# Score products in two phases, GpSimd's work in layer 0 moved, v and a gate product in native float32

## The chip, the core and the metric

One core of a Trainium2 chip runs the kernel. The metric is device time in microseconds (us) of one launch. Five queues work beside each other: TensorE (products, written to the accumulator banks), VectorE, ScalarE and GpSimd (elementwise work) and SyncE (DMA from main memory).

## What is computed

Two layers on 256 tokens of width 1,024, all float32. Layer 0 mixes tokens by an RWKV-7 recurrence, layer 1 by causal attention; each is followed by a dense gated network and each sub-layer by a LayerNorm. The change touches layer 0's mixer:

```
xx = time_shift(x) - x
xr, xw, xk, xv, xa, xg = [x + xx * mu[n] for n in range(6)]
r, k, v = xr @ w_r, xk @ w_k, xv @ w_v
w = -softplus(-(w0 + tanh(xw @ w1) @ w2)) - 0.5
a = sigmoid(a0 + (xa @ a1) @ a2)
g = sigmoid(xg @ g1) @ g2
kk = k * k_k, each head divided by its norm
k = k * (1 + (a - 1) * k_a)
per token: S = S * decay + (S @ -kk) kk*a + v k ;  y = S @ r
out = (group_norm(y) + bonus(r, k, v)) * g @ w_o
```

## The kernel before

The recurrence runs in four chunks of 64 tokens. Within a chunk all pairs of tokens meet in score matrices: for each of the 16 heads, keys and removal keys (tile `KB`, 128 columns: 64 of each) are multiplied with the scaled `-kk` and the scaled r (tile `AR`, 64 columns of each). The part with `-kk` is a triangular matrix that must be inverted before the recurrence can begin. `scores(q)` (line 876) makes both parts in one product of 128 columns per head and chunk, sixteen per group q of four heads. VectorE multiplies each bank with the causal mask into `SC`, and ScalarE copies the 32-wide diagonal blocks to `LD`. It begins when `KB` is whole (`kb`), and r has been scaled (`ar`).

`inverse` (line 951) waits for all `ld` events, transposes `LD` to `LT` on VectorE and then runs 31 short steps of a product `tmp` and a sum `TT`. It ends with the transposes `TN` and `LD`. `merge` (line 996) builds 64-wide inverses out of the 32-wide ones by small TensorE products named `n` and `t`. Between the two it asks `fill` for a number of v products (lines 1000 to 1020); with `FREE = 10` the first of these requests is met only after eleven of the sixteen parts of v's second half. Then `recurrence` (line 1036) runs steps z, u, s and y per chunk and half of the heads. `stacked` builds `AZ`, `bonus` scales `v` on GpSimd with the bonus sums `sb`.

Float32 weights go through `Stream` (line 101) in tiles of 128 rows by 1,024. A "split" tile is loaded into one of three `raw` buffers, rounded by ScalarE to `hi`, and its rest `lo` is taken by VectorE or GpSimd; a product is then three fast ones (hi with hi, lo with hi, hi with lo). Table `PL` (line 69) says which tiles' `lo` go to GpSimd. A "native" tile is loaded into a slot and multiplied as float32 directly, slower per column but with no split. "stack" is a smaller split, and "raw" a native tile that lies in a raw buffer.

```
OFF = ('ka', 'kk1', 'xxv')
PL = {..., 'k': [2], 'r': [0], 'v': [2, 3, 4, 5, 6, 7], 'g2': [0, 1], ...}
MIXV = 'pool'
MIXG = 'pool'
for n, (ww, xx) in enumerate(((w[0], xh), (w[1], xh), (w[0], xl))):
    mm(ps, xx[:, k % 4, TOK[hf]], ww[:, kk, :], ...)
```

These are OFF, the operations that GpSimd has in layer 0 (the scaling `ka` in `weigh`, one half of `KB` in `keys`, the rest of the split of xv), and who makes the inputs xv and xg in `mix` (line 649), and `v_part` (line 1222), the three products of v. The gate's second product has four products per block of 128 columns, 32 in all.

The order on every queue is set when the program is built. `Issue.run` (line 357) plays the program on `Clock` (line 197), a table of costs per engine; of the parts that are ready by it, the one with the lowest rank goes next. `dense0` (line 1259), the row of large products k, r, v, g and o, has rank 30, the last. So a change of a cost, of a rank or of the work moves instructions everywhere. Each engine then executes its instructions strictly in this order.

Of the kernel before, what the change touches and what calls it, by code (L numbers as in the profile page):

```python
# [99 lines left out]

class Stream:
# [29 lines left out]
    def run(self):  # L131
        for i, (name, kind, a, b, rows, src) in enumerate(self.specs):
# [61 lines left out]
class Clock:  # L194


    def __init__(self):
# [42 lines left out]
    def charge(self, eng, op, args, kw):  # L240
# [9 lines left out]
        elif eng == "PE":  # L250
# [8 lines left out]
            late = 0.197
        elif eng == "DVE":  # L260
            cost, late = 0.068 + n / (1920.0 if op == "tensor_scalar" and not psum else 960.0) * (6 if op == "reciprocal" else 1), 0.128
            cost += 0.0625 * sum(x.free_size() == 1 for x in srcs if n > 1)
# [1517 lines left out]
```

## Time and profile before

| what | value |
|---|---|
| median of 3 runs | 745.94 us (743.14 to 745.95) |
| the profiled execution | 744.11 us, its span 742.3 us |
| busy TensorE, VectorE, ScalarE, GpSimd | 684.7, 535.8, 389.8, 186.9 us |
| share of the chain of waits, TensorE, VectorE, ScalarE | 66%, 21%, 4% |
| mean granted TensorE clock | 0.967 of 2.4 GHz |

The busy time of TensorE holds waits inside its pipeline, so 92% busy doesn't say that it bounds everything; which engine bounds a stretch is read from the chain of waits and from the idle time in front of single rows. All rows carry line 300, a helper; the names of the tiles tell the operation. Times of a row are from the span's start.

### The profile page before, as it was taken

The numbers are of one execution on the slowest core, as the hardware profiler recorded it, in microseconds if no ns is written. First come the engines' busy times: TensorE is split into PE (matmuls) and PEld (weight loads), VectorE is DVE, ScalarE is ACT, GpSimd is POOL, SyncE is SP. The second block draws the span as 40 slices with busy tenths as digits, with TensorE's granted clock in tenths as the row PEclk, the third lists the DMA queues.
The fourth block names the chain that finished last, engine by engine and source line by source line (L and its number), as shares of the span: only waits on it lengthen the run. The fifth ranks groups of instructions, "written<-read, shape, count | busy, mean of one in ns | idle before, by whom it ended". The sixth has DMA issues, their size and how long they took to land.

```text
span 742.3 us, 11807 instructions
## 1 busy us (share of the span) xinstructions
PE 684.7 (92%) x4500; PEld 585.5 (79%) x4500; DVE 535.8 (72%) x912; ACT 389.8 (53%) x711; POOL 186.9 (25%) x132
## 2 busy tenths in 40 slices
PE   6899797898878999999999699999979999999995
PEld 5799796777657888888888478777769888888885
DVE  7989999839997756655666935977686656666576
ACT  5864445465344555455456424756636554545560
POOL 5677956451462100000000713113040000000000
PEclk9989889899999999999999999999999999999998
DMA  6445213030545655555557615345056555555541
GB/s 243 153 143 192 90 47 114 30 115 33 174 168 187 226 194 178 196 190 185 192 191 216 233 48 179 126 142 200 28 170 197 189 188 194 180 189 197 179 164 57
DMA packets 33577, 117.21 MB, mean 158 GB/s; under 512 B 3808, under 2 KB 4832, under 8 KB 33520
## 3 DMA queue, kind: packets, MB, share of 16 engines
q1 hardware_dynamic: 31936, 110.89, 44.6%
q10 hardware_dynamic: 1584, 5.57, 2.3%
q8 instruction: 35, 0.57, 0.3%
q14 instruction: 22, 0.18, 0.1%
HBM read 115.40 MB, written 1.05 MB: 157 GB/s over the span
## 4 chain that ended last, share of the span: by engine, by line
PE 66%; DVE 21%; ACT 4%; issue 4%; DMA 2%; POOL 1%; DVEq 0%; SPq 0%; ACTq 0%; POOLq 0%
PE gu L300 29%; PE acc L300 14%; PE qkv L300 9%; DVE xtok L300 3%; DVE TT L300 3%; PE gn L300 2%; DVE lo L300 2%; DVE tmp L300 2%; PE o L300 2%; PE sc L300 2%; DVE xlo L300 1%; DVE mx L300 1%; PE tr L300 1%; PE k L300 1%; POOL lo L300 1%
## 5 line engine op out<-in xcount | busy, mean ns | idle before, releaser
L300 DVE TENSOR_TENSOR lo<-raw,hi 128x1024 fp32r<-128x1024 f32 (+1 forms) x172 | 210.7, 1231 | 151.4 <-ACT hi L300 151.0
L300 ACT CAST hi<-raw 128x1024 fp32r<-128x1024 f32 (+1 forms) x214 | 212.1, 999 | 175.7 <-issue 75.9
L300 PE MATMUL gu<-xw,hi 128*128 128x512 f32 x640 | 225.9, 393 | 0.0
L300 PE MATMUL gu<-xw,lo 128*128 128x256 f32 x640 | 180.3, 282 | 0.0
L300 POOL TENSOR_TENSOR lo<-raw,hi 128x1024 fp32r<-128x1024 f32 (+1 forms) x41 | 89.0, 2185 | 245.2 <-ACT hi L300 232.7
L300 PEld LDWEIGHTS gu<-xw,hi 128*128 128x128 f32 x640 | 120.1, 188 | 26.5
L300 PEld LDWEIGHTS gu<-xw,lo 128*128 128x128 f32 x640 | 120.3, 188 | 0.8
L300 PE MATMUL acc<-hi,hh 128*128 128x512 f32 (+1 forms) x180 | 53.7, 368 | 0.0
L300 PE MATMUL acc<-lo,hh 128*128 128x512 f32 (+1 forms) x180 | 53.7, 368 | 0.0
L300 PE MATMUL acc<-hi,hl 128*128 128x512 f32 (+1 forms) x180 | 53.6, 367 | 0.0
L300 PE MATMUL qkv<-hi,xhi 128*128 128x512 f32 x96 | 39.5, 412 | 0.5 <-ACT xhi L300 0.5
L300 ACT ACTIVATE silu<-silu 128x256 f32<-128x256 f32 x40 | 16.7, 417 | 44.0 <-DVE silu L300 44.0
L300 PE MATMUL qkv<-hi,xlo 128*128 128x512 f32 x96 | 38.0, 396 | 0.6 <-DVE xlo L300 0.6
L300 PE MATMUL qkv<-lo,xhi 128*128 128x512 f32 x96 | 38.1, 396 | 0.0
L300 PEld LDWEIGHTS acc<-hi,hl 128*128 128x128 f32 x180 | 32.7, 188 | 6.3 <-DVE hl L300 0.2
L300 PEld LDWEIGHTS acc<-lo,hh 128*128 128x128 f32 x180 | 32.7, 188 | 5.8
L300 PEld LDWEIGHTS acc<-hi,hh 128*128 128x128 f32 x180 | 31.7, 188 | 6.0 <-ACT hh L300 0.2
L300 PE MATMUL o<-hi,xhi 128*128 128x512 f32 x64 | 27.7, 436 | 2.8 <-ACT xhi L300 2.8
L300 PE MATMUL o<-lo,xhi 128*128 128x512 f32 x64 | 27.1, 423 | 2.0 <-POOL lo L300 2.0
L300 PE MATMUL o<-hi,xlo 128*128 128x512 f32 x64 | 27.0, 428 | 0.9 <-DVE xlo L300 0.9
L300 POOL TENSOR_TENSOR ro<-ro 128x512 f32<-128x512 f32 x8 | 12.1, 1513 | 55.9 <-DVE ro L300 55.9
L300 PE MATMUL gn<-hi,xw 128*128 128x256 f32 x128 | 24.8, 290 | 0.1
(229 smaller groups left out, 1291.4 us busy)
## 6 DMA issues: line engine op xcount, KB each, us to landing
raw<-in_w_in_dram SPq DMA_DIRECT2D x80, 512.0 KB, 3.4
raw<-in_w_dn_dram SPq DMA_DIRECT2D x44, 512.0 KB, 3.4
raw<-in_w_qkv_dram SPq DMA_DIRECT2D x24, 512.0 KB, 3.3
raw<-in_w_o_dram SPq DMA_DIRECT2D x20, 512.0 KB, 3.4
raw<-in_w_r_dram SPq DMA_DIRECT2D x8, 512.0 KB, 3.5
raw<-in_w_v_dram SPq DMA_DIRECT2D x8, 512.0 KB, 3.6
raw<-in_w_if_dram SPq DMA_DIRECT2D x8, 512.0 KB, 3.3
raw<-in_w_k_dram SPq DMA_DIRECT2D x6, 512.0 KB, 3.8
```

The costliest lines, as they stand in the source:

```text
L300: ins = f(*args, **kw).ins
```

## The change

Seven edits, all for layer 0 up to the recurrence, and new costs in the planner.

1. `scores(q, n)` has two phases. Phase 0 needs only `KB` and the `-kk` part of `AR`. It makes products of 64 columns into two banks, with the two halves of rows in turn, feeds `LD` and is masked into `SC`. Phase 1 multiplies with r's part, into a tile of its own, `SR`, which only step y reads. Ranks are 3 and 5.
2. `OFF` is empty. Both halves of `KB` are VectorE's, and `ka` is an activation with scale and bias on ScalarE.
3. Inputs xv and xg are made on VectorE, eight steps of 256 elements each (on GpSimd it was eight operations of 512 for each).
4. v's weights are native: the first half in raw buffers, the second in `lo` buffers. xv isn't split.
5. The gate's second product is native, with one block of 128 and one of 32 rows (before, 96 rows held the 32 three times). Its activations aren't split.
6. The splits of k and r on GpSimd go to VectorE. `selrk` is one operation instead of eight.
7. The planner prices the port that VectorE and GpSimd share, a change of the number of rows on TensorE, scans and fast products differently.

```
-OFF = ('ka', 'kk1', 'xxv')
+OFF = ()
 MIXR = 'dve'
 MIXA = "dve"
 BON = 'pool'
 BONW = 'T'
 ORDERED = False
-PL = {'wo1': [5, 6, 7], 'in1': [0, 1, 2, 3], 'qkv': [1, 3, 4, 5, 6, 7, 11], 'wo0': [1, 2, 4, 6, 7, 9, 10], 'k': [2], 'r': [0], 'v': [2, 3, 4, 5, 6, 7], 'g2': [0, 1], 'w2': [], 'in0': [0, 2, 3, 5]}
+PL = {'wo1': [5, 6, 7], 'in1': [0, 1, 2, 3], 'qkv': [1, 3, 4, 5, 6, 7, 11], 'wo0': [1, 2, 4, 6, 7, 9, 10], 'in0': [0, 2, 3, 5]}
 LD = {}
-MIXV = 'pool'
-MIXG = 'pool'
+MIXV = 'dve'
+MIXG = 'dve'
...
+NATIVE = ("native", "in hi", "in lo")
...
+            elif kind in NATIVE:
+                raw = self.wp.tile([128, 1024], F32R, tag=kind[3:], name=f"nat{i}", bufs=SPL).bitcast(F32)
...
-                cols, cost = n, n / 2388.0
+                cols, cost = n, n / 2388.0 + 0.014
             else:
-                cols, cost = 4 * n, max(n / 588.0, m / 600.0) if not beside else max(0.027, m / 1200.0)
+                rows = self.region(aps[1])[1][:2]
+                turn = rows[1] - rows[0] <= 64 and self.rows not in (None, rows)
+                self.rows = rows
+                cols, cost = 4 * n, max(n / 588.0, m / 600.0) if not beside and not turn else max(0.027, m / 1200.0)
             late = 0.197
+            k = aps[1].partition_size()
+            shape = 32 if k <= 32 else 64 if k <= 64 else 128
+            if self.shape not in (None, shape):
+                cost += SWITCH
+            self.shape = shape
...
+            wide = [x for x in srcs if x.free_size() > 1 or n == 1]
+            if eng == "POOL" and op != "memset" or eng == "DVE" and not psum and (
+                    len(wide) > 1 or op in ("tensor_scalar", "tensor_copy")):
+                start = self.shared(eng, start, cost)
...
-    s2("v", "w_v", 0)
+    s2("v", "w_v", 0, "raw")
     s1("g1", "w_g1a", 0, "native")
-    s1("g1", "w_g1b", 0, "native", 96)
-    specs.append(("g2", "split", 1, 1024, 128, a["w_g2a"]))
-    specs.append(("g2", "stack", 1, 1024, 96, a["w_g2b"]))
-    s2("v", "w_v", 1)
+    s1("g1", "w_g1b", 0, "native", 32)
+    specs.append(("g2", "in hi", 1, 1024, 128, a["w_g2a"]))
+    specs.append(("g2", "in hi", 1, 1024, 32, a["w_g2b"]))
+    s2("v", "w_v", 1, "in lo")
...
-            on("ka").tensor_scalar(w[:, j, :], av[g][:, o + j, :], vec[:, KA + p:KA + p + 1], omka[:, p:p + 1],
-                              ALU.mult, ALU.add)
+            act.activation(w[:, j, :], av[g][:, o + j, :], AF.Identity, scale=vec[:, KA + p:KA + p + 1],
+                           bias=omka[:, p:p + 1])
+        yield w
+        yield I.idle("DVE")
...
-    def scores(q):
+    def scores(q, n):
 
         yield ev(f"kb{q}")
-        yield ev(f"ar{q}")
-        yield ev("SC")
-        fin = count(4, lambda: I.reach(ev(f"sc{q}"), SC[:, :, q * 2:q * 2 + 2]))
-        left = count(4, lambda: I.reach(ev(f"ld{q}"), LD))
-
-        def done(j, hp, ps):
-            for d in range(2):
-                r, h = 64 * (1 - hp) + 32 * d, (q * 2 + j) * NC
-                act.copy(out=LD[r:r + 32, h:h + NC, :],
-                         in_=ps[r:r + 32].rearrange("p (c t) -> p c t", c=NC)[:, :, 32 * d:32 * d + 32])
-            left()
-            dve.tensor_tensor(SC[:, hp, q * 2 + j], ps.rearrange("p (c t) -> p c t", c=NC),
-                              mask[:, None, :].to_broadcast([128, NC, 128]), ALU.mult)
+        if n == 1:
+            yield ev(f"ar{q}")
+        yield ev(("SC", "SR")[n])
+        dst = (SC, SR)[n]
+        fin = count(2, lambda: I.reach(ev(f"{('sc', 'sr')[n]}{q}"), dst[:, :, q * 2:q * 2 + 2]))
+        left = count(2, lambda: I.reach(ev(f"ld{q}"), LD))
+
+        def done(hp, ps):
+            if n == 0:
+                for d in range(2):
+                    r = 64 * (1 - hp) + 32 * d
+                    act.copy(out=LD[r:r + 32, q * 8:q * 8 + 8, :],
+                             in_=ps[r:r + 32].rearrange("p a c t -> p (a c) t")[:, :, 32 * d:32 * d + 32])
+                left()
+            dve.tensor_tensor(dst[:, hp, q * 2:q * 2 + 2], ps,
+                              mask[:, None, None, n * C:n * C + C].to_broadcast([128, 2, NC, C]), ALU.mult)
             fin()
 
+        ps = [bank("sc").rearrange("p (a c t) -> p a c t", a=2, c=NC) for _ in HALF]
         for j in range(2):
-            for hp in range(2):
-                rs = HALF[hp]
-                ps = bank("sc")
-                for c in range(NC):
-                    mm(ps[:, c * 128:(c + 1) * 128], KB[q][rs, j, c].rearrange("p o t -> p (o t)"),
-                       AR[q][rs, j, c].rearrange("p o t -> p (o t)"), True, True)
-                I.after(ps, done, j, hp, ps)
-                yield 0.0
+            for c in range(NC):
+                for hp, rs in enumerate(HALF):
+                    mm(ps[hp][:, j, c, :], KB[q][rs, j, c].rearrange("p o t -> p (o t)"), AR[q][rs, j, c, n, :], True, True)
+        for hp in range(2):
+            I.after(ps[hp], done, hp, ps[hp])
...
+            for q in (2 * f, 2 * f + 1):
+                yield ev(f"sr{q}")
...
-                mm(y[vr, ds], SC[:, hp, p, c, 64:128], UV[c][:, hp, p, :], start=(c == 0), stop=True,
+                mm(y[vr, ds], SR[:, hp, p, c, :], UV[c][:, hp, p, :], start=(c == 0), stop=True,
...
-            xh, xl = mixed["xv"][k // 4]
-            for n, (ww, xx) in enumerate(((w[0], xh), (w[1], xh), (w[0], xl))):
-                mm(ps, xx[:, k % 4, TOK[hf]], ww[:, kk, :], start=(k + n == 0), stop=(k + n == KT + 1))
+            mm(ps, mixed["xv"][k // 4][:, k % 4, TOK[hf]], w[:, kk, :], start=(k == 0), stop=(k == KT - 1))
...
-        x = half_slot("sg")[:rows, 0, :]
-        act.activation(x, ps[:rows, :T], AF.Sigmoid)
-        yield x
-        act.copy(out=hgs[:rows, n * 2, :], in_=x)
-        yield hgs[:rows, n * 2, :]
-        if n == 0:
-            dve.tensor_tensor(hgs[:, 1, :], x, hgs[:, 0, :].bitcast(F32), ALU.subtract)
-        else:
-            dve.tensor_tensor(hgs[32:64, 2, :], x[32:64], hgs[32:64, 2, :].bitcast(F32), ALU.subtract)
-        I.reach(ev(f"hg{n}"), hgs[:rows, n:n * 2 + 1, :] if n else hgs[:, 0:2, :])
+        act.activation(hgs[:rows, n, :], ps[:rows, :T], AF.Sigmoid)
+        I.reach(ev(f"hg{n}"), hgs[:rows, n, :])
...
-                mix(3, "xv", 3, slot, eng=dict(pool=pool, dve=dve)[MIXV])
-        early.close()
-        scp = l0.enter_context(tc.tile_pool(name="scp", bufs=1))
-        SC = scp.tile([128, 2, KT, NC, 128], F32, name="SC")
-        SCh = SC.rearrange("p a h c t -> p a (h c) t")
-        LD = scp.tile([128, 32, 32], F32, name="LD")
-        I.reach(ev("SC"))
+                mix(3, "xv", 3, eng=dict(pool=pool, dve=dve)[MIXV])
+        early_r.close()
+        srp = l0.enter_context(tc.tile_pool(name="srp", bufs=1, side="right"))
+        SR = srp.tile([128, 2, KT, NC, C], F32, name="SR")
+        I.reach(ev("SR"))
...
-                for n, (ww, xx_) in enumerate(((g2[0][0], hgs[:, 0, :]), (g2[0][1], hgs[:, 0, :]), (g2[0][0], hgs[:, 1, :]),
-                                               (g2[1][0], hgs[:96, 2, :]))):
-                    mm(ps[:, j * T:(j + 1) * T], ww[:, 0, p * 128:(p + 1) * 128], xx_, start=(n == 0), stop=(n == 3))
+                for n, rows in enumerate((128, 32)):
+                    mm(ps[:, j * T:(j + 1) * T], g2[n][:, 0, p * 128:(p + 1) * 128], hgs[:rows, n, :], n == 0, n == 1)
...
-        for p in range(KT):
-            pool.tensor_scalar(selrk[:, p, :], sel2, vec[:, RK + p:RK + p + 1], None, ALU.mult)
+        pool.tensor_tensor(selrk, sel2[:, None, :].to_broadcast([128, KT, 2]),
+                           vec[:, RK:RK + KT, None].to_broadcast([128, KT, 2]), ALU.mult)
...
-        I.add(4, scores(q))
+        I.add(3, scores(q, 0))
+        I.add(5, scores(q, 1))
```

`shared`, called there, delays the one engine in the plan while the other holds the port.

How the order moves, at the three places that the prediction speaks of:

VectorE at the start of the inverse. `SC` and `SR` are masks, `AR` and `rk` are r's rows, `mix` is xv. Before:

```order
L300 TENSOR_TENSOR SC<-sc_1096,cst 128x512
L300 TENSOR_TENSOR SC<-sc_1104,cst 128x512
L300 STREAM_TRANSPOSE LT_165<-LD 128x32x32
L300 TENSOR_TENSOR tmp<-LT_165,TT_166 128x31
L300 TENSOR_TENSOR TT_166<-TT_166,tmp 128x31
L300 TENSOR_TENSOR tmp<-LT_165,TT_166 128x60
L300 TENSOR_TENSOR TT_166<-TT_166,tmp 128x2x30
```

With the change:

```order
L337 TENSOR_TENSOR SC<-sc_904,cst 128x512
L337 TENSOR_TENSOR SC<-sc_905,cst 128x512
L337 TENSOR_TENSOR rk_991<-r_705,k_119 128x512
L337 STREAM_TRANSPOSE LT_168<-LD 128x32x32
L337 TENSOR_TENSOR AR_125<-r_806,G_117 128x8x64
L337 TENSOR_TENSOR tmp<-LT_168,TT_169 128x31
L337 TENSOR_TENSOR rk_1029<-r_806,k_120 128x512
L337 TENSOR_TENSOR TT_169<-TT_169,tmp 128x31
L337 SCALAR_TENSOR_TENSOR mix_1025<-xx_110,vec,xT_84 128x256
L337 TENSOR_TENSOR tmp<-LT_168,TT_169 128x60
```

In all eight masks precede `LT`; before there were sixteen. Rows of r and of xv now stand between the steps of the inverse, and further down so do `SR` and xg.

TensorE between the inverse and the recurrence: `n` and `t` belong to the merge, `hg` is the gate's activation. Before, the end of the gate's product:

```order
L300 MATMUL g_1441<-hg_151,hi_1304 128x256
L300 MATMUL g_1441<-hg_151,hi_1273 128x256
L300 MATMUL g_1441<-hg_151,lo_1274 128x256
L300 MATMUL g_1441<-hg_151,hi_1273 128x256
L300 MATMUL n_1421<-TN_167,SC 32x32 x16
L300 MATMUL n_1422<-TN_167,SC 32x32 x32
L300 MATMUL g_1441<-hg_151,hi_1304 128x256
L300 MATMUL v_1543<-hi_1343,xhi_865 128x512
L300 MATMUL v_1543<-lo_1344,xhi_865 128x512
L300 MATMUL v_1543<-hi_1343,xlo_866 128x512
L300 MATMUL v_1543<-hi_1343,xhi_865 128x512
L300 MATMUL n_1421<-TN_167,SC 32x32 x16
```

With the change, the same place:

```order
L337 MATMUL g_1349<-mix_1203,nat_1224 32x256 x4
L337 MATMUL g_1349<-mix_1204,nat_1224 32x256 x4
L337 MATMUL n_1363<-TN_170,SC 32x32 x16
L337 MATMUL n_1364<-TN_170,SC 32x32 x32
L337 MATMUL g_1443<-hg_154,nat_1226 128x256
L337 MATMUL n_1363<-TN_170,SC 32x32 x16
L337 MATMUL g_1443<-hg_154,nat_1228 128x256
L337 MATMUL g_1443<-hg_154,nat_1226 128x256
L337 MATMUL g_1443<-hg_154,nat_1228 128x256
```

The gate's second product stood ahead of the first `n` but for its last row; now all sixteen of its products stand behind the first 48 of `n`. Eleven native v products follow and then the first `t`.

ScalarE before the decay `G`: `E` and `a` are sigmoids, `kkr` is the scaled k. Before:

```order
L300 ACTIVATE a_109<-z_346,vec 128x256 x2
L300 ACTIVATE a_109<-z_353,vec 128x256 x2
L300 ACTIVATE a_110<-z_360,vec 128x256 x2
L300 ACTIVATE sq_375<-kkr_118 128x512
L300 CAST hi_386<-raw_265 128x1024
L300 ACTIVATE a_110<-z_367,vec 128x256 x2
L300 ACT_TABLE_LOAD
L300 ACTIVATE G_113<-E_111 128x16x64
```

With the change:

```order
L337 ACTIVATE sq_361<-kkr_121 128x512
L337 CAST hi_376<-raw_261 128x1024
L337 ACTIVATE a_113<-z_353,vec 128x256 x2
L337 CAST xhi_208<-mx_229 128x512
L337 CAST xhi_208<-mx_230 128x512
L337 ACTIVATE ka_424<-a_112,omka,vec 128x256 x2
L337 ACTIVATE kkr_121<-k_331,vec 128x256 x2
L337 ACTIVATE ka_451<-a_112,omka,vec 128x256 x2
L337 ACT_TABLE_LOAD
L337 ACTIVATE G_116<-E_114 128x16x64
```

Four `ka` scalings and two casts of xr's pieces now stand ahead of the table load and `G`.

## Rows read from the trace of the kernel before

**Rows 1.** Chain of waits: start us, length us, what was worked on, count.
```profile
148.44 3.51 PE v L300 x14
...
151.96 2.14 PE t L300 x64
...
242.81 4.21 PE gu L300 x24
```

**Rows 2.** Stages: us, busy us per engine, granted PE clock, DMA share, GB/s.
```profile
45.30:52.10 6.80, 6.80 (x35) 6.80 (x34) 6.72 (x7) 3.19 (x4) 6.15 (x4) 0.51 0.69 230
...
103.20:110.20 7.00, 7.00 (x23) 5.84 (x23) 6.49 (x24) 0.18 (x1) 0.79 (x1) 0.52 0.00 1
...
125.50:132.70 7.20, 0.32 (x3) 0.12 (x1) 7.19 (x37) 0.78 (x2) 0.00 (x0) 0.86 0.22 73
```

**Rows 3.** Timeline of VectorE, layer 0: start, us, operation, count, idle before, releaser.
```profile
15.72 0.87 DVE L300 SCALAR_TENSOR_TENSOR mx<-xx,vec,xT 128x256 f32<-128x256 f32 x2
...
66.92 1.28 DVE L300 TENSOR_TENSOR kkr<-kkr,rb 128x512 f32<-128x512 f32 x2
...
77.09 0.74 DVE L300 SCALAR_TENSOR_TENSOR AR<-kkr,G 128x256 f32<-128x256 f32 x2
...
92.22 4.26 DVE L300 TENSOR_TENSOR SC<-sc,cst 128x512 f32<-128x512 f32 x7
...
99.82 2.13 DVE L300 STREAM_TRANSPOSE LT<-LD 128x1024 f32<-128x1024 f32 x1
...
102.84 1.19 DVE L300 TENSOR_TENSOR TT<-TT,tmp 128x31 f32<-128x31 f32 x1
...
110.96 0.47 DVE L300 TENSOR_TENSOR tmp<-LT,TT 128x160 f32<-128x160 f32 x2
...
111.35 2.67 DVE L300 TENSOR_TENSOR TT<-TT,tmp 128x160 f32<-128x160 f32 x2
...
122.43 2.64 DVE L300 TENSOR_TENSOR tmp<-LT,TT 128x128 f32<-128x128 f32 x2
...
132.24 0.41 DVE L300 TENSOR_TENSOR hg<-sg,hg 128x256 fp32r<-128x256 f32 x1
...
136.51 2.05 DVE L300 STREAM_TRANSPOSE TN<-TT 128x1024 f32<-128x1024 f32 x1
```

**Rows 4.** Timeline of GpSimd during the inverse.
```profile
111.49 2.43 POOL L300 TENSOR_TENSOR lo<-raw,hi 128x1024 fp32r<-128x1024 f32 x1 [7.50 <-ACT hi L300]
...
119.63 2.13 POOL L300 TENSOR_TENSOR v<-v,sb 128x512 f32<-128x512 f32 x2
...
122.46 2.47 POOL L300 TENSOR_TENSOR lo<-raw,hi 128x1024 fp32r<-128x1024 f32 x1 [0.70 <-ACT hi L300]
```

**Rows 5.** Timeline of ScalarE in the head.
```profile
26.09 1.05 ACT L300 CAST hi<-raw 128x1024 fp32r<-128x1024 f32 x1 [1.83 <-DMA raw<-in_w_k_dram]
...
31.27 2.39 ACT L300 ACTIVATE a<-z,vec 128x256 f32<-128x256 f32 x6
```

**Rows 6.** Timeline of TensorE in layer 0 (f32 products are two instructions each).
```profile
26.21 0.39 PE L300 MATMUL z<-lr,hi 128*128 128x256 f32 x1 [3.23 <-DVE lr L300]
...
79.03 0.38 PE L300 MATMUL r<-xhi,lo 128*128 128x256 f32 x1 [2.78 <-DVE lo L300]
...
88.26 6.02 PE L300 MATMUL sc<-AR,KB 64*128 64x128 f32 x56 [1.44 <-DVE rk L300]
...
118.52 7.07 PE L300 MATMUL g<-mix,nat 128*128 128x256 f32 x32
...
138.73 3.12 PE L300 MATMUL n<-TN,SC 32*32 32x32 f32 x96
...
144.16 0.50 PE L300 MATMUL v<-lo,xhi 128*128 128x512 f32 x1
...
144.49 0.39 PE L300 MATMUL v<-hi,xlo 128*128 128x512 f32 x1
...
158.64 0.68 PE L300 MATMUL z<-UV,SC 64*64 64x64 f32 x16
```

More of the change, by code (lines that the diff above doesn't have):

```diff
@@ L43 @@
 TICK, WARM = 10.24 / 3, 3060
+SWITCH = 0.2
 MARGIN = 0.85
@@ L114, in load @@
     def load(self, upto):
-        while self.nl < len(self.specs) and (self.nl < upto or self.specs[self.nl][1] == "native"):
+        while self.nl < len(self.specs) and (self.nl < upto or self.specs[self.nl][1] in NATIVE):
             i = self.nl
@@ L122, in load @@
             v = raw[:rows, :a * b].rearrange("p (a b) -> p a b", a=a)
-            if kind != "native":
+            if kind not in NATIVE:
                 self.ring.append(i)
@@ L139, in run @@
             r = self.raw.pop(i)
-            if kind in ("native", "raw"):
+            if kind in NATIVE + ("raw",):
                 self.sp[i] = r
@@ L201, in __init__, with shared @@
         self.columns = {}
+        self.port, self.shape, self.rows = {"DVE": [], "POOL": []}, None, None
+    def shared(self, eng, t, cost):
+        other = "POOL" if eng == "DVE" else "DVE"
+        for s, e in self.port[other]:
+            if s <= t < e:
+                t = e
+                break
+        later = [s for s, e in self.port[other] if t <= s < t + cost]
+        if later:
+            d = t + cost - min(later)
+            self.port[other] = [(s + d, e + d) if s >= t else (s, e) for s, e in self.port[other]]
+            self.free[other] = self.free.get(other, 0.0) + d
+        self.port[eng].append((t, t + cost))
+        return t
     @staticmethod
@@ L262, in charge @@
             cost += 0.0625 * sum(x.free_size() == 1 for x in srcs if n > 1)
+            if op == "tensor_tensor_scan":
+                cost *= 1.7
         elif eng == "ACT":
@@ L269, in charge @@
         else:
-            cost, late = (0.036 + 0.0009 * n if op == "memset" else 0.15 + 0.0021 * n), 0.155
+            cost, late = (0.036 + 0.0009 * n if op == "memset" else 0.1 + 0.001 * n if op == "tensor_copy" else
+                          0.1 + 0.0017 * n if op == "tensor_scalar" else 0.1 + 0.0021 * n), 0.155
         if eng == "DMA":
@@ L434, in trunk @@
     l0 = ctx.enter_context(ExitStack())
-    early = ctx.enter_context(ExitStack())
-    ep = early.enter_context(tc.tile_pool(name="ep", bufs=8))
+    early, early_r = ctx.enter_context(ExitStack()), ctx.enter_context(ExitStack())
+    epr = early_r.enter_context(tc.tile_pool(name="epr", bufs=4, side="right"))
+    ep = early.enter_context(tc.tile_pool(name="ep", bufs=4))
     uid, pools = [0], {}
@@ L451, in early_slot, with early_slot_r @@
         return ep.tile([128] + shape, dtype, tag="e4", name=nm(name))
+    def early_slot_r(shape, name, dtype=F32):
+        return epr.tile([128] + shape, dtype, tag="er", name=nm(name))
     def half_slot(name, dtype=F32):
@@ L928, in stacked @@
             vr, ur = HALF[hp], HALF[1 - hp]
-            act.copy(out=AZ[q][vr, :, hp, 1:], in_=SC[vr, hp, q * 2:q * 2 + 2, 1:, 0:64])
+            act.copy(out=AZ[q][vr, :, hp, 1:], in_=SC[vr, hp, q * 2:q * 2 + 2, 1:, :])
             yield AZ[q][vr, :, hp, 1:]
@@ L1259, in dense0 @@
     def dense0():
-        nonlocal SC, SCh, LD
+        nonlocal SC, SCh, LD, SR
         yield eps_ln
@@ L1288, in dense0 @@
                         I.reach(ev(f"w2{n}"))
+        early.close()
+        scp = l0.enter_context(tc.tile_pool(name="scp", bufs=1))
+        SC = scp.tile([128, 2, KT, NC, C], F32, name="SC")
+        SCh = SC.rearrange("p a h c t -> p a (h c) t")
+        LD = scp.tile([128, 32, 32], F32, name="LD")
+        I.reach(ev("SC"))
         yield ev("xr")
@@ L1314, in dense0 @@
         yield ev("xg")
-        for n, rows in enumerate((128, 96)):
+        for n, rows in enumerate((128, 32)):
             w = yield from W.get("g1")
@@ L1329, in dense0 @@
                 p = u * 2 + j
-                for n, (ww, xx_) in enumerate(((g2[0][0], hgs[:, 0, :]), (g2[0][1], hgs[:, 0, :]), (g2[0][0], hgs[:, 1, :]),
-                                               (g2[1][0], hgs[:96, 2, :]))):
-                    mm(ps[:, j * T:(j + 1) * T], ww[:, 0, p * 128:(p + 1) * 128], xx_, start=(n == 0), stop=(n == 3))
+                for n, rows in enumerate((128, 32)):
+                    mm(ps[:, j * T:(j + 1) * T], g2[n][:, 0, p * 128:(p + 1) * 128], hgs[:rows, n, :], n == 0, n == 1)
                 yield 0.0
@@ L1744, in _layout @@
     d["w_2"] = np.stack([np.concatenate([w, w], axis=0) for w in (inp["rwkv_w2"][0], inp["rwkv_a2"][0])])
[L1745 to L1746 removed]
+    d["w_g1a"], d["w_g1b"] = s1(inp["rwkv_g1"][0][:, :128]), s1(inp["rwkv_g1"][0][:, 128:], 32)
+    d["w_g2a"], d["w_g2b"] = inp["rwkv_g2"][0][:128], inp["rwkv_g2"][0][128:]
     d["w_o0"], d["w_o1"], d["w_qkv"] = s2(inp["rwkv_w_o"][0]), s2(inp["moba_w_o"][0]), s2(inp["moba_w_qkv"][0])
```

13 lines of the change are left out of this document (5 added, 8 removed).

## The prediction

> **What bounds the kernel now.** I read the chain of waits first. From 243 us to the end it is almost only TensorE's products, in blocks like the first of [rows 1], and the change alters no operation there; what it can gain or lose lies in layer 0, before 237 us. There the chain changes hands. Up to 100 us it is mostly VectorE, from 100 to 136 us it is the inverse on VectorE alone, and from 137 us on it is TensorE with ScalarE's and GpSimd's splits, such as fourteen rows of v and the merge products `t` [rows 1].
>
> The stage table shows what TensorE did meanwhile [rows 2]: it was granted half speed (0.51 and 0.52) from 45.3 to 52.1 and from 103.2 to 110.2 us, and between 125.5 and 132.7 us it worked 0.32 of 7.2 us, waiting for the gate's split `hg`.
>
> VectorE's own rows [rows 3] show the disease that the change treats. A pair of inverse steps over 160 elements takes 0.47 us at 110.96 and 2.67 us at 111.35; at that moment GpSimd starts a split of 2.43 us [rows 4]. Five pairs (first and last in [rows 3]) take 12.8 us where five times 0.47 is 2.4: 10.4 us lost, against 12.0 us of GpSimd work (five rows, three of them shown [rows 4]). So VectorE loses 0.87 us for each us that GpSimd works. The first step of the inverse (31 elements, 1.19 us) loses about another 1.0.
>
> **How one row counts.** Seven masks in a row take 4.26 us, one row of that size 0.67: rows overlap by 0.07, so a 512-element row costs 0.60 us, a mix step of 256 elements 0.40 (0.87 for two), an `AR` step 0.34 (0.74 for two) [rows 3]; a split of 1,024 elements I count twice a mask less the overlap, 1.1.
>
> **Part 1: the head, up to the norms `rb` (66.9 us).** Without GpSimd's work VectorE delivers the low-rank activations sooner; TensorE waited 3.23 us for them before its first `z` [rows 6]. Of that ScalarE keeps about half, since its cast at 26.09 us waited for a DMA whose buffer VectorE frees [rows 5]. Against it stand six operations new in the stretch before ScalarE's `G`: two casts moved ahead of it and four `ka` scalings, about 0.4 us each by the sigmoids (2.39 us for six [rows 5]): 2.4 us on the engine that the chain runs through there. As much is lost as won, and the splits of k that wait behind them come no earlier. I take **+0.5 us**; the ends are -2 (ScalarE has the slack after all) and +3 (TensorE's longer wait for these splits brings another half-speed stretch like that at 45.3 us, which lost 3.4 of 6.8).
>
> **Part 2: from `rb` to the inverse.** Before, VectorE needed from 66.92 to 99.82 us [rows 3]. Now it has, by its order: four `kkr`, eight halves of `KB` (four of them GpSimd's before), eight masks of the first phase, one `AR` for r and one `rk`, 22 rows of 0.60, so 13.2; eight `AR` steps, 2.7; one split, 1.1. The other r rows, eight masks and two v splits come later or never. That is 17.0 us, with no GpSimd work beside it, and the transpose `LT` starts at 83.9: **-15.9**. The scores are ready by then: 28 products took 6.02 us, 0.21 each [rows 6], and a product half as wide can cost between half of that and, if something other than its columns bounds it, all of it; the last sixteen end within about 1 us of the masks' turn in both cases. Ends: 1.5 either way.
>
> **Part 3: the inverse.** `LT` to `TN` took 36.7 us (99.82 to 136.51). Off go the 11.4 us lost to GpSimd and two `hg` rows of 0.4, new among the steps come two `AR`, two `rk`, eight `SR` masks (12 times 0.60) and sixteen mix steps (0.40): 13.6 us. GpSimd keeps one piece of work that meets it, the two `v` rows of 2.13 us [rows 4], at 0.87: 1.8 us. Sum 39.9, **+3.2**: the work moved off GpSimd costs VectorE what the stalls cost before. Ends -2 (no meeting with `v`) and +1.5 (the last `AR` waits for r).
>
> **Part 4: from `TN` to the recurrence.** `TN` now starts at 124.3 us and the products `n` follow as before. From `n` to the first `z` of the recurrence TensorE took 19.9 us (138.73 to 158.64 [rows 6]). In its new order stand, between these two: 64 products `n` (3.12 us for 48, so 4.2), 64 `t` (2.14 for 32, so 4.3 [rows 1]), all sixteen native products of g and fourteen of v. Sixteen native 256-column products take 7.07 us with the last one's tail [rows 6], 0.43 each; the v products have twice the columns, 0.86. That is 6.9 and 12.0. And eight times g changes from 128 rows of weights to 32 and back. The row after such a change took 0.50 us, its neighbour 0.39 [rows 6]: sixteen times 0.11 is 1.8. Sum 29.2, **+9.3**. Before, most of the gate's products were done while the inverse still ran; now they stand behind `n`, and `t` waits for eleven v products by construction (the merge asks for fillers).
>
> On those changes a page has a rule that speaks against this edit: the Trainium skill, TensorEngine Tiling (Array Packing), section Key Properties, says that changing the tiling mode drains the engine. The trace agrees in kind, with the 0.11 us; without such a price the sum would be 1.8 us lower, and I keep the row's price.
>
> **Part 5: after `z`.** The recurrence, group norm and o product have the same operations; two native v products (1.7 us) stand where nine rows of 0.25 stood (2.3; 3.51 us for fourteen [rows 1]). The splits given to GpSimd there and later are the same, and the stretch from there to the feed-forward part I take as moving whole. Planner costs moved some rows past each other in attention; 0, with 3 us either way.
>
> **Sum.** +0.5 - 15.9 + 3.2 + 9.3 = -2.9 us, against the profiled execution's own 744.1: **741.2 us**. That execution lies 1.8 us under the median of the runs shown (745.9). About 0.5%, 3.7 us, is what a measurement here can tell from no change.
>
> **The rivals.**
>
> *The head gains and the switches are free.* If ScalarE has slack (part 1 at -2), `v` misses the inverse (-1.8) and g's changes of rows cost nothing (-1.8), the sum is -9: 735 us. For it: the chain leaves ScalarE whenever a raw tile arrives in time. Against: the 0.50 us row.
>
> *TensorE is already the second runner.* From the end of `rb` to the end of the first g product it took 66.9 to 125.6 us, 58.7 us [rows 3, 6], with 3.5 lost to half speed in the 7.0 us at 103.2 [rows 2] and 2.8 and 1.4 in two waits for VectorE [rows 6]. Native v costs sixteen times 0.86 instead of 48 times 0.25, 1.8 more. If all the waits and the slow clock come back, it reaches `n` at 127.4, while `TN` allows 126.5: 0.9 us late, and with a head 2 us worse than I took nothing is won: 744.1 us. For it: bonus sums and scores still precede v. Against: its waits in that stretch were for VectorE, which now runs ahead.
>
> *The native products run at half speed, and it gets slower.* The first sixteen v products at half speed take 27.5 us, 13.8 more. Without the waits and the slow clock TensorE would be 6.8 us early at `n` (58.7 - 7.7 + 1.8 from 66.9, against 126.5), so `z` comes 7.0 later than I say: 748.2 us. It decides once more than 9.7 us are lost (the lead and my 2.9), 19 us of these products at the lower clock. For it: exactly this place had 0.52 before, behind the bonus sums [rows 2]. Against: it came back to full speed after 7 us, and native products leave no gaps.
>
> *The first phase starts no earlier than the whole did.* It would need a mask or a load copy that waits for r; VectorE's order has none ahead of `LT` but one `AR` and one `rk`, whose r is early. Then 757 us; I give it 2 in 100.
>
> **How the numbers follow.** My forecast 0.42, with its own spread from 738 to 745; the first rival 0.22, the second 0.20, the third 0.13, the last 0.02, a hundredth for the rest. Faster by over 0.5% means under 740.4: the first rival and half of my forecast's case, 0.43. Slower, above 747.8: the third and the last, 0.15. The rest, 0.42, is the same. The range takes in the first rival with a little of the head (734) and the third (749); likeliest alone, 738 to 745.
>
> **What would show it.** Right: `LT` near 84 us, `TN` near 124, `n` to `z` near 29 us, `z` near 156, and no inverse pair above 0.6 us except where `v` meets it. Part 1 is wrong if `rb` lands before 65 or after 70 us. Part 3 is wrong if small steps still show rows of 2 us. Part 4 is wrong if `n` starts well after `TN` ends, with the granted clock near 0.5 over the v products. A gain or loss that only appears after 240 us would mean that the planner's new costs, and not the edits in layer 0, made the difference.

## The result and the profile after

With the change the kernel takes **762.8 us** (761.28 to 764.12, four runs), 1.0234 times as long as before (95% interval 1.0203 to 1.0265): 17 us slower, where 3 us faster was forecast. The profiled execution took 761.28 us, its span 759.5 us.

From the page of the changed kernel (the totals per engine, the granted clock in 40 slices of 19 us, and the shares of the chain):

```profile
span 759.5 us, 11910 instructions
PE 711.0 (94%) x4596; PEld 587.5 (77%) x4596; DVE 512.8 (68%) x930; ACT 378.1 (50%) x687; POOL 106.0 (14%) x83
...
PEclk9989999589999999999999999999989999999998
...
PE 77%; DVE 13%; ACT 4%; issue 2%; DMA 2%; POOL 1%; SPq 0%; DVEq 0%; ACTq 0%; POOLq 0%
```

GpSimd works 106 us instead of 187 and VectorE 513 instead of 536, so the work did move. TensorE is busy for 26 us more, and the chain's share on VectorE fell from 21 to 13% while TensorE's rose from 66 to 77%. One slice of the clock stands out, the eighth, at 0.5 of full speed: 133 to 152 us.

VectorE in the timeline of the changed kernel, at the anchors of [rows 3]:

```profile
67.95 1.27 DVE L337 TENSOR_TENSOR kkr<-kkr,rb 128x512 f32<-128x512 f32 x2
...
85.32 1.46 DVE L337 TENSOR_TENSOR SC<-sc,cst 128x512 f32<-128x512 f32 x2 [1.17 <-ACT LD L337]
...
87.28 2.03 DVE L337 STREAM_TRANSPOSE LT<-LD 128x1024 f32<-128x1024 f32 x1
...
97.73 0.69 DVE L337 TENSOR_TENSOR AR<-r,G 128x512 f32<-128x512 f32 x1 [2.94 <-PE r L337]
...
118.89 1.31 DVE L337 TENSOR_TENSOR TT<-TT,tmp 128x176 f32<-128x176 f32 x2
...
121.56 1.26 DVE L337 TENSOR_TENSOR tmp<-LT,TT 128x128 f32<-128x128 f32 x2
...
128.05 1.90 DVE L337 STREAM_TRANSPOSE TN<-TT 128x1024 f32<-128x1024 f32 x1
```

The first `kkr` starts 1.0 us later than before, `LT` 12.5 us earlier and `TN` 8.5 us earlier. Up to here the change does what it says. GpSimd's two rows in that stretch:

```profile
118.91 1.22 POOL L337 TENSOR_TENSOR v<-v,sb 128x512 f32<-128x512 f32 x1 [75.39 <-DVE tmp L337]
121.56 1.18 POOL L337 TENSOR_TENSOR v<-v,sb 128x512 f32<-128x512 f32 x1 [1.44 <-PE g L337]
```

They begin with the only two pairs of the inverse's later half that take 1.3 us instead of 0.45: 1.7 us lost for 2.4 us of GpSimd work, 0.7 per us. A second piece of GpSimd work meets the inverse, which the prediction did not have: the copies to `AZ`, 2.6 us from 125.23 us on. In the kernel before they began at 136.29 us, behind the inverse's last step. Beside them four more pairs take 0.55 to 0.67 us instead of 0.3, 1.2 us lost.

TensorE after the inverse, to the first `z` of the recurrence (a native float32 product is two instructions):

```profile
130.10 4.83 PE L337 MATMUL n<-TN,SC 32*32 32x32 f32 x96 [3.27 <-DVE TN L337]
134.86 1.22 PE L337 MATMUL g<-hg,nat 128*128 128x256 f32 x2
136.01 1.91 PE L337 MATMUL n<-TN,SC 32*32 32x32 f32 x32
137.86 17.32 PE L337 MATMUL g<-hg,nat 32*128 32x256 f32 x30
155.10 11.05 PE L337 MATMUL v<-nat,mix 128*128 128x512 f32 x22
166.08 2.21 PE L337 MATMUL t<-LD,TN 32*32 32x32 f32 x64
...
173.33 0.68 PE L337 MATMUL z<-UV,SC 64*64 64x64 f32 x16
```

And the same stretch by windows (the figure after the busy times is the granted clock):

```profile
126.80:130.10 3.30, 0.03 (x1) 0.03 (x1) 3.27 (x8) 0.37 (x1) 1.51 (x3) 1.00 0.00 0
130.10:137.90 7.80, 7.79 (x131) 7.02 (x131) 5.05 (x5) 1.73 (x3) 2.80 (x3) 0.53 0.01 2
137.90:155.10 17.20, 17.20 (x31) 7.44 (x30) 0.00 (x0) 4.18 (x8) 0.00 (x0) 0.50 0.00 0
155.10:157.70 2.60, 2.60 (x4) 1.18 (x4) 0.00 (x0) 2.48 (x6) 0.00 (x0) 0.50 0.00 0
157.70:173.30 15.60, 15.60 (x154) 8.60 (x152) 1.29 (x2) 5.78 (x13) 3.52 (x3) 1.00 0.14 41
```

TensorE stood idle for 3.3 us in front of `n`, was then granted 1.2 GHz (0.50) from 130.5 to 157.7 us, and worked through all of it. The gate's sixteen products took 18.4 us (1.15 and 17.24). `n` to `z` is 43.2 us, where the same stretch before was 19.9 [rows 6]: the stretch takes 23.3 us more, which eats the 8.5 us won at `TN` and puts `z` 14.7 us later than before. The feed-forward part, which began at 242.81 us [rows 1], begins here at 256.25.

### The profile page after: what moved, and what is told of

Same layout as the page of the kernel before. It is cut to its first block, busy times and chain, and to the rows that moved or that the text cites. A ratio compares the mean times of both kernels' runs of the same rounds, so it can differ in the third digit from the quotient of the medians.

```text
span 759.5 us, 11910 instructions
## 1 busy us (share of the span) xinstructions
PE 711.0 (94%) x4596; PEld 587.5 (77%) x4596; DVE 512.8 (68%) x930; ACT 378.1 (50%) x687; POOL 106.0 (14%) x83
## 4 chain that ended last, share of the span: by engine, by line
PE 77%; DVE 13%; ACT 4%; issue 2%; DMA 2%; POOL 1%; SPq 0%; DVEq 0%; ACTq 0%; POOLq 0%
PE gu L337 29%; PE acc L337 14%; PE qkv L337 7%; PE o L337 5%; DVE xtok L337 4%; PE r L337 3%; PE g L337 2%; PE sc L337 2%; PE gn L337 2%; PE v L337 2%; PE tr L337 1%; DVE TT L337 1%; DVE tmp L337 1%; PE pv L337 1%; PE k L337 1%
## 5 line engine op out<-in xcount | busy, mean ns | idle before, releaser
L337 ACT CAST hi<-raw 128x1024 fp32r<-128x1024 f32 (+1 forms) x204 | 201.6, 996 | 171.2 <-issue 74.6
L337 POOL TENSOR_TENSOR lo<-raw,hi 128x1024 fp32r<-128x1024 f32 (+1 forms) x32 | 65.1, 2054 | 237.7 <-ACT hi L337 230.0
L337 PEld LDWEIGHTS acc<-hi,hl 128*128 128x128 f32 x180 | 32.8, 188 | 6.1
L337 PEld LDWEIGHTS acc<-hi,hh 128*128 128x128 f32 x180 | 31.7, 188 | 6.0
L337 PE MATMUL o<-hi,xhi 128*128 128x512 f32 x64 | 28.3, 443 | 3.2 <-DVE gmv L337 3.1
L337 PE MATMUL tr<-cst,xtok 128*128 128x128 f32 x48 | 9.5, 340 | 14.4 <-DVE xtok L337 10.5
```

The source lines that it names most:

```text
L337: ins = f(*args, **kw).ins
```

## The experiments

Two theories on the half-speed stretch came first. **A**: the gate's products of 128 and 32 rows in turn hold TensorE at the lower clock. **B**: idle time lowers the clock, it returns when it will, and the turns cost only a drain each. The kernel before was timed again with each group of runs, at 745.8 to 746.9 us.

### 1. The gate filled up to 128 rows

```
-    s1("g1", "w_g1b", 0, "native", 32)
+    s1("g1", "w_g1b", 0, "native")
...
-                for n, rows in enumerate((128, 32)):
+                for n, rows in enumerate((128, 128)):
...
-    d["w_g2a"], d["w_g2b"] = inp["rwkv_g2"][0][:128], inp["rwkv_g2"][0][128:]
+    d["w_g2a"], d["w_g2b"] = inp["rwkv_g2"][0][:128], np.pad(inp["rwkv_g2"][0][128:], ((0, 96), (0, 0)))
```

The gate's first product makes four copies of its last 32 activations, and three of them meet the zeros.

> The 32 rows of the gate's second product are filled up to 128 with rows of zero weights: as many products and columns, but TensorE never changes between 128 and 32 rows there. Theory A (the alternation holds TensorE at the lower clock, its idle time before n only started it): the sixteen products take 16 x 0.43 = 7 us where they took 18.4, granted clock near 1.0 before they end; n to z falls from 43.2 to about 31 us, time about 750. Theory B (the clock fell in the idle time and comes back when it will, whatever rows are multiplied; the alternation costs only its drains): 16 x 0.86 = 13.8 us at 0.50, z 4.6 us earlier, time about 758. Theory C (rows don't matter at all): 762.8, as with the change.

Measured 750.88 us (ratio 1.0048, 1.0018 to 1.0077), 12 us under the change (the profiled execution lies 4.7 us under this median, so stretches are compared here and not totals). The order on TensorE is the same up to the first `t`. The first row of `n`, and then the windows of this run behind it:

```profile
128.41 3.09 PE L337 MATMUL n<-TN,SC 32*32 32x32 f32 x96 [0.57 <-DVE TN L337]
```

```profile
128.40:133.50 5.10, 5.09 (x130) 4.67 (x130) 5.01 (x5) 1.73 (x3) 3.76 (x6) 0.92 0.01 3
133.50:139.60 6.10, 6.10 (x17) 4.90 (x16) 0.08 (x1) 1.16 (x2) 0.00 (x0) 0.51 0.00 0
139.60:143.00 3.40, 3.40 (x17) 3.01 (x16) 0.00 (x0) 2.08 (x5) 0.00 (x0) 1.00 0.00 0
```

The clock still falls behind `n`, but is back at 139.6 us, in the middle of the gate. The products take 10.2 us instead of 18.4, `n` to `z` (128.41 to 160.11) 31.7 us. The stretch and the time are theory A's (31 and 750 us); the products' 10.2 us lie between its 7 and B's 13.8. But two things differ from the change here: TensorE also stood idle for only 0.6 us ahead of `n`, and not for 3.3. Runs 2 and 5 have no turns either, behind a wait of the full length.

### 2. The 32-row products left out

```
-                for n, rows in enumerate((128, 32)):
-                    mm(ps[:, j * T:(j + 1) * T], g2[n][:, 0, p * 128:(p + 1) * 128], hgs[:rows, n, :], n == 0, n == 1)
+                mm(ps[:, j * T:(j + 1) * T], g2[0][:, 0, p * 128:(p + 1) * 128], hgs[:, 0, :], True, True)
```

> Leaves out the eight products of 32 rows (the gate lacks its last 32 hidden values). Theory A: eight products of 128 rows, 8 x 0.43 = 3.4 us and the clock back to 1.0 within a few us of n's end; z 15 us earlier, time about 748. Theory B: the clock stays at 0.50 for as long as with the change (until about 157 us), the eight products take 6.9 us and the first v products run at half speed too, 0.86 us lost on each; z about 8 us earlier, time about 755.

One execution, of a kernel whose gate lacks its last 32 activations: 745.01 us. TensorE's rows:

```profile
129.86 4.54 PE L337 MATMUL n<-TN,SC 32*32 32x32 f32 x96 [3.33 <-DVE TN L337]
134.33 1.22 PE L337 MATMUL g<-hg,nat 128*128 128x256 f32 x2
...
137.33 5.06 PE L337 MATMUL g<-hg,nat 128*128 128x256 f32 x14
...
159.31 0.68 PE L337 MATMUL z<-UV,SC 64*64 64x64 f32 x16
```

The idle time before `n` is the same 3.3 us, yet the clock is back near 141 us, sixteen us sooner than with the change, and all of v runs at 1.0. The eight products took 6.1 us, nearer to B's 6.9 than to A's 3.4, since most of them ran before the clock was back. So it is A for the long stretch, and for the first ten us what stands ahead of it, idle time and `n`. These two are not told apart; with 0.6 us of idle time (run 1) the clock fell some 4 us after `n` began, with 3.3 (the change) 0.5 us after.

### 3. The gate ahead of n

```
         yield ev(f"TN{hp}")
+        yield ev("g")
```

> The merge waits for the gate, so that the same sixteen products of 128 and 32 rows stand before n, where TensorE idled for 3.3 us; nothing else moves. Theory B (idle time starts the low clock, rows don't matter): the clock doesn't fall, the gate takes 6.9 us and its drains, n starts near 136 at 1.0, z near 157 us, time about 746. Theory A (alternation lowers the clock by itself or holds it): the gate's products run at 0.50 from some point on although TensorE was busy before, about 14 to 18 us, n starts at 141 to 146, z at 165 to 170, time 754 to 760.

Measured 751.82 us (1.0068, 1.0043 to 1.0093). The gate's row, and the stretch by windows:

```profile
126.24 9.71 PE L337 MATMUL g<-hg,nat 128*128 128x256 f32 x32
```

```profile
126.20:135.90 9.70, 9.70 (x34) 4.91 (x33) 8.41 (x13) 3.90 (x8) 4.31 (x6) 1.00 0.00 0
135.90:141.60 5.70, 5.70 (x103) 3.96 (x102) 0.00 (x0) 3.30 (x8) 0.00 (x0) 0.98 0.01 3
141.60:148.00 6.40, 6.40 (x39) 3.47 (x38) 0.00 (x0) 2.52 (x5) 0.00 (x0) 0.50 0.00 0
```

Neither theory had it right. The gate in turns holds 1.0 over 9.6 us, 0.60 us a product, and needs 2.7 us more than the 6.9 that its products take when all have 128 rows (run 9): 0.17 per change of rows at full speed, where I had 0.11. The clock falls near 141.5 us, without idle time, over `n` and v.

### 4. The gate behind v

In `dense0` the block of v's second half goes ahead of the gate's, and so do its weights:

```
-    specs.append(("g2", "in hi", 1, 1024, 128, a["w_g2a"]))
-    specs.append(("g2", "in hi", 1, 1024, 32, a["w_g2b"]))
     s2("v", "w_v", 1, "in lo")
+    specs.append(("g2", "in hi", 1, 1024, 128, a["w_g2a"]))
+    specs.append(("g2", "in hi", 1, 1024, 32, a["w_g2b"]))
```

> The gate's second product stands behind v's second half, so that v's 128-row products follow n directly; rows and products are the same. Theory A: the clock is back some 3 us after v begins; n to z is 43.2 less 18.4 for the gate and less about 2, 23 us; z near 153; the gate's products lie in gaps of the recurrence and cost 0 to 8 us of its end; time 743 to 750. Theory B: v runs at 0.50 until about 157 us, z near 160; time 752 or more.

Measured 755.32 us (1.0114, 1.0082 to 1.0146). `n` to `z` is 26.2 us (130.02 to 156.23), the clock back at about 142.5, so it does come back over v's rows, as theory A said. But the time is not A's 743 to 750, since the gate is not hidden between the recurrence's steps: from `z` to the end of the first long feed-forward row is 110.9 us, where the change has 100.0. I had allowed 8 us for that.

### 5. Old planner costs from the attention layer on

With the gate filled up; `charge_old` is the cost function before the change.

```
     def dense1(xs, xtok):
+        I.clk.charge = I.clk.charge_old
```

> The kernel with the gate filled up to 128 rows, and the planner's old costs for everything from the attention layer on; layer 0 stays as it was there. Theory P (the new costs order the attention worse): the first feed-forward row to the second one's takes 318.3 us again, as before the change, where the filled-up gate had 321.8; time 3.5 us lower, about 747.4. Rival (the attention is longer for another reason, such as where the weight loads stand when it starts): 321.8 stays, time 751.

Measured 746.61 us (0.9984, 0.9958 to 1.0009). The chain of run 1, then that of this run:

```profile
245.72 12.53 PE gu L337 x72
...
566.07 13.95 PE gu L337 x80
```

```profile
250.32 12.55 PE gu L386 x72
...
569.16 12.56 PE gu L386 x72
```

From the end of the one row to the end of the other: 321.8 us with the new costs, 318.9 with the old. 2.9 us of that stretch, and 4.3 by the medians, are the planner's and have nothing to do with the edits in layer 0. The other traces agree: this stretch takes 320.8 to 323.7 us in the change and in runs 1, 3, 4, 6, 7 and 8, which have the new costs there, and 318.1 to 320.0 us before and in runs 5 and 9 to 12, which have the old ones.

This trace also settles what run 1 left open. Up to the attention it is run 1's program, but in this execution TensorE waited ahead of `n` as long as with the change and 0.5 us more:

```profile
130.73 4.79 PE L386 MATMUL n<-TN,SC 32*32 32x32 f32 x96 [3.77 <-DVE TN L386]
135.44 1.22 PE L386 MATMUL g<-hg,nat 128*128 128x256 f32 x2
...
138.44 8.21 PE L386 MATMUL g<-hg,nat 128*128 128x256 f32 x30
```

The clock falls about 131 us, under `n`, and is back near 141.4 us. The sixteen products take 9.2 us, and `n` to `z` 32.8. So behind the same wait the turns cost the gate 9.2 us more, and they keep the clock down for another 16 us.

### 6 and 7. v split again; v and the gate split again

```
-    s2("v", "w_v", 0, "raw")
+    s2("v", "w_v", 0)
...
-    s2("v", "w_v", 1, "in lo")
+    s2("v", "w_v", 1)
```

With these come back the three products in `v_part`, the split of xv, and v's six entries in `PL`. In run 7 the gate's weights and activations are split as before the change too.

> v's weights and xv are split again, six of the eight rests on GpSimd; the gate stays native with its 128 and 32 rows. The planner then puts the gate's products ahead of n, so TensorE isn't idle there and the clock holds at 1.0 over them (theory A); v's rows cost 0.25 us each again. But GpSimd's splits meet the inverse again: some five of them, 2.4 us at 0.87 lost per us, so TN about 10 us later than with the change, at 138; n to z about 20; z near 160; time 748 to 752. If native v, and not the gate, had cost the time, it would be under 744.

> Both v and the gate's second product are split again: what the two phases and the other work taken off GpSimd do alone. TensorE has 32 rows of 0.12 us for the gate (3.9) instead of 9.7 us, and 0.25 us rows for v. TN near 138 as above, n to z about 20 us, z near 158, time 745 to 749 with the attention's 3.3 us in it. If the two phases are worth what the masks weigh (some 10 us), and the splits don't meet the inverse, TN is near 130 and the time under 740.

Measured 758.53 us (1.0168) and 758.06 us (1.0164). Both misses: `TN` came at 147.3 and 148.2 us. VectorE and TensorE in run 6:

```profile
104.66 2.12 DVE L337 STREAM_TRANSPOSE LT<-LD 128x1024 f32<-128x1024 f32 x1
```

```profile
125.91 14.08 PE L337 MATMUL g<-hg,nat 128*128 128x256 f32 x32
```

The inverse starts 17 us later than with the change. In the order that this planner makes, more rows stand ahead of it on VectorE: xv and its rests (`mx`, `xlo`), some 5.6 us, six of the masks `SR` and rows of r, with 4.5 us of waits between them. GpSimd's splits of v meet the inverse again, and it takes 42.6 us (40.8 with the change) although those rows are out of it. So native v is part of what lets the inverse start early. Run 6 holds a second thing, by windows from the gate's first row on:

```profile
125.90:130.60 4.70, 4.70 (x17) 2.52 (x16) 4.67 (x25) 0.96 (x2) 0.00 (x0) 0.97 0.30 112
130.60:139.90 9.30, 9.30 (x17) 4.00 (x16) 9.27 (x50) 2.19 (x3) 0.00 (x0) 0.50 0.00 0
...
143.50:146.00 2.50, 2.50 (x11) 2.04 (x10) 2.50 (x5) 0.00 (x0) 2.09 (x1) 0.91 0.63 210
```

The gate in turns begins at full speed after 12 us without idle time, falls to 0.50 some 4.5 us later and stays there until v's 128-row products have run for some 3.6 us. So the clock can fall over turns of 128 and 32 rows without idle time ahead of them. In run 3 it did not fall over the same sixteen products; why not is open.

### 8. No v products asked for ahead of t

With the gate filled up:

```
-FREE = 10
+FREE = 16
```

> The gate filled up to 128 rows, and the merge no longer asks for v products (FREE = 16), so that t follows n, and the rest of the gate and of v stand between the steps of the recurrence. Theory G (the recurrence waits on other engines for some 6 us that TensorE can fill): z near 140, the recurrence about 11 us longer than 29, its end some 9 us earlier, time about 742. Rival (TensorE is the bound from n to the end of the recurrence, and the clock falls among its small rows): no gain or some loss, 750 to 756.

Measured 753.1 us (1.0108, 1.0077 to 1.0138): the rival.

```profile
128.00:150.00 22.00, 21.91 (x287) 17.93 (x288) 4.89 (x5) 8.33 (x16) 2.09 (x5) 0.53 0.01 1
150.00:164.00 14.00, 14.00 (x57) 7.81 (x55) 0.95 (x2) 6.13 (x13) 1.04 (x1) 1.00 0.00 0
```

The first products of `z` do come at 147.9 us. But `n`, `t` and single gate products follow each other at 0.53 for 22 us, and the clock is back near 149.8 us, where the gate's products have begun to come two in a row.

### 9. Three repairs together

The edits of runs 1, 3 and 5 in one kernel: the gate filled up, ahead of `n`, and the old planner costs from the attention on.

> Three repairs together: the gate filled up to 128 rows, its products ahead of n (the merge waits for the gate), and the old planner costs from the attention layer on. Theory A: no alternation and no idle time ahead of n, so the gate's sixteen products take 7 us at 1.0 and lie in TensorE's wait of 3.8 us for the inverse; n to z falls, z 3 to 4 us earlier than in the run without the second repair (163.6), time 742.5 to 744. Rival (the clock falls among n's small products whatever stands ahead of them, and what the gate wins n and v lose): 746 to 747, no gain over that run.

Measured **740.01 us** (0.9933, 0.9908 to 0.9958), more than I had expected.

```profile
127.28 7.07 PE L386 MATMUL g<-hg,nat 128*128 128x256 f32 x32
...
136.86 3.12 PE L386 MATMUL n<-TN,SC 32*32 32x32 f32 x96
...
155.54 0.68 PE L386 MATMUL z<-UV,SC 64*64 64x64 f32 x16
```

```profile
127.20:134.20 7.00, 7.00 (x35) 6.15 (x34) 6.92 (x14) 3.09 (x7) 2.52 (x5) 1.00 0.00 0
134.20:155.50 21.30, 21.30 (x285) 13.07 (x283) 3.55 (x5) 11.36 (x24) 5.29 (x5) 1.00 0.09 32
```

The gate takes 6.9 us and the clock never leaves 1.0, over `n` either. In this stretch run 3 differs by the 32-row products and by one v product that stands behind the first `n` and not ahead: from the gate's first row to `z` it needed 34.2 us, this run 28.3. Of the 6.0 between them 2.7 are the changes of rows and 3.2 the half of 6.4 us at 0.50.

### 10 and 11. Fewer v products ahead of z, and v between the groups of n

On top of run 9, `FREE = 6` in both; in run 11 the merge also asks for a v product behind each group:

```
         for q, hs in parts:
...
-        yield from fill(FILLI[hp])
+            yield from fill(1)
```

> As the run before, but with FREE = 6: ten v products ahead of the recurrence's first z instead of fourteen, the others between its steps. If the recurrence waits long enough for other engines, four products of 0.86 us are hidden there: z 3.4 us earlier and 2 to 3.4 us off the time, about 741. Rival (the steps of the recurrence follow each other at TensorE's pace, or v's buffers then hold up the splits of the o weights): z is earlier but the recurrence longer by as much, no gain, 743 to 746.

> As the run before, with v products of 128 rows between the groups of n's small products. If small products in a row are what makes the clock fall, it holds at 1.0 through the merge, which saves the 4 us that the kernel with the gate first lost between 141 and 148 us: 738 to 741. Rival (the clock falls all the same, as n and t still are most of the stretch's time): no gain over the run before.

Run 10: 740.75 us (0.9933, 0.9912 to 0.9954). `z` comes 3.8 us earlier than in run 9, at 151.8, and the time is the same: its rival, no gain. Run 11: **736.45 us** (0.9885, 0.9855 to 0.9915), the fastest. Not by the mechanism named, as the clock was 1.0 over the merge in run 10 already. A later window of run 10, then of run 11:

```profile
215.00:240.00 25.00, 21.64 (x143) 19.58 (x144) 19.26 (x27) 12.57 (x21) 9.02 (x4) 0.93 0.53 180
```

```profile
215.00:240.00 25.00, 23.89 (x165) 21.56 (x166) 19.21 (x30) 13.90 (x24) 7.17 (x3) 1.00 0.64 206
```

Run 11 has no slow clock from 215 to 240 us, over the last o products and the LayerNorm, and TensorE does more in that window. What in the new order brings this about is open.

### 12. The kernel before with the last repairs

The edits of runs 3 and 11 on the kernel before, with nothing of the change:

```
-FREE = 10
+FREE = 6
...
+        yield ev("g")
...
-        yield from fill(FILLI[hp])
+            yield from fill(1)
```

> The kernel before with the last two repairs alone: the merge waits for the gate, v products stand between the groups of n, and FREE = 6. Theory D (what the repaired kernel gains over the one before comes from the change: the inverse ends some 8 us earlier, and TensorE has had no idle time): the inverse still ends near 138 us here, TensorE still waits some 10 us for it, and the time is 743 to 747, no gain beyond the order of v. Rival (the gain is the order of v and n, which the old kernel could have had alone): 737 to 740.

Measured 745.43 us (0.9997, 0.998 to 1.0013). Theory D, with no gain by the order of v and `n` alone:

```profile
136.81 2.07 DVE L300 STREAM_TRANSPOSE TN<-TT 128x1024 f32<-128x1024 f32 x1
```

```profile
126.00:138.00 12.00, 4.95 (x24) 4.69 (x25) 11.80 (x63) 0.91 (x2) 1.01 (x2) 0.57 0.00 0
```

`TN` stands where it stood, and TensorE works 5 of the 12 us before it. So the order alone is not what runs 9 to 11 gain over the kernel before; they need the change. That it is the earlier inverse, which leaves no such wait, fits these rows, but no run separates it from the rest of the change.

## Why the prediction was wrong

The span grew by 17.2 us; the forecast was -2.9. Point by point:

- **Part 1**, `rb`: +0.5 forecast, +1.0 measured. Right in the number, but by luck in part: the first `z` came 3.5 us earlier (22.70 and 26.21 us), of which ScalarE kept 0.7 at `E` and not half, and its first `G` came 3.0 us later (40.14 and 37.16 us). Why only 1.0 of that reached `rb` was not followed.
- **Part 2**, to `LT`: 17.0 us forecast, 19.3 measured, against 32.9 before. The halves of `KB` cost 0.70 each and not 0.60, and VectorE waited 1.2 us for ScalarE's copies of the last scores to `LD` (the row at 85.32). Right in kind, though outside its ends of 1.5 us.
- **Part 3**, the inverse: 39.9 forecast, 40.8 measured. The work that left GpSimd did cost VectorE what the stalls had cost before, and the one wait for r (2.9 us in the row at 97.73) was about twice what my upper end allowed. The copies to `AZ` cost 1.2 us more that I did not have.
- **Part 4**, `n` to `z`: 29.2 forecast, 43.2 measured. **This step failed.** 9.7 of the 14.0 us are the gate: 18.4 us for sixteen products, where I had 6.9 and 1.8 for changes of rows. `n` took 6.6 instead of 4.2, v 13.9 instead of 12.0, `t` the 4.3 forecast. Every duration in that sum came from a row at 2.4 GHz ("0.43 each"), while the place was one where TensorE had just waited for the inverse. The sign that I had named for a failure here, `n` well after `TN`, did not come: `TN` ended at 129.95 us and `n` began at 130.10. At 1.2 GHz a product costs 0.86 (in run 1, from 134.1 to 139.2 us, 0.43 for each of its two instructions), and 0.29 more for each change of rows, which makes 1.15. Runs 1 and 5 take the turns away and the stretch falls to 31.7 and 32.8 us; run 2, with eight products fewer, has 29.5, and run 9, with the gate moved ahead, 18.7.
- **Part 5**, after `z`: 0 forecast; -1.3 us measured up to the feed-forward part, then +3.8 up to the end. "Planner costs moved rows past each other in attention; 0" was wrong, and the +3.8 lie outside its 3 us; run 5 shows that these costs are the cause of about 3.

-2.9 and 0.5, 2.3, 0.9, 14.0, -1.3 and 3.8 make 17.3. The order of the misses is plain: without turns the change is 4 us slower than before (run 1), without the attention's share as fast (run 5).

The **third rival** named the mechanism, native products at half speed and a slower kernel, with a price of 13.8 us. But it put it on v's first half, ahead of `n`, where the clock was 1.0 all through (from 87 to 130 us), and let the lead at `n` absorb 7 us of it. Behind `n` nothing absorbs it. I had the row for it: the windows from 125.5 us [rows 2] show TensorE idle in that very place before, and the trace has what came of it: behind that wait, from 132.7 to 138.7 us, the gate's split products ran at a granted clock of 0.59. The **second rival** was wrong: TensorE ended the gate's first products at 126.8 us and waited 3.3 us for `TN`. The **first rival**'s free changes of rows don't exist. On those the Trainium skill, TensorEngine Tiling (Array Packing), section Key Properties, says that a change of the tiling mode drains the engine: the runs agree, with 0.17 us at 2.4 and 0.29 us at 1.2 GHz. So the rule was the right warning, but of the gate's 9.7 us over the forecast the turns' own price at full speed is only some 0.9 (2.7 where I had 1.8); the rest is the lower clock.

## What to carry to other kernels

Work that a change moves behind a wait must be priced at both clocks: look at the granted clock of the rows that stand there now, and add the doubled time to the range. Give TensorE products with all rows, filled up with zeros if need be, and put them ahead of a wait and not behind it: the same sixteen products cost 18.4 us behind `n` with 128 and 32 rows in turn, 10.2 and 9.2 with 128 (runs 1 and 5), and 6.9 ahead of it. A change of a planner's costs is a change of every stage, so time it apart.

## What was not expected of the hardware

TensorE's clock fell without any idle time: in run 6 it went from 1.0 to 0.50 some 4.5 us into products of 128 and 32 rows in turn, and stayed there to the end of those products and 3.6 us beyond. In run 3 the same turns held 1.0 for 9.6 us and the fall came at about 141.5 us, between the groups of `n`. With 128 rows ahead (run 9) `n`, which has 32, ran at 1.0. Whether it is the drains or the unused rows that count was not told apart, as runs 1 and 2 take both away. And VectorE's two-input rows lost 0.7 us per us of GpSimd work beside them, where the five pairs before gave 0.87 [rows 3, 4]; beside the copies to `AZ` it was 0.5.
